# Row sums and row picks on the full TensorE array, padded with zeros, in a four-layer decoder trunk

## The chip, the cores and the metric

The kernel runs on one core of one Trainium2 chip. The metric is the device time of one execution in microseconds: 1587.0 us is the median of three executions of the kernel before (1582.32 to 1587.86). The profile is of one further execution.

## The reference

A decoder of four layers works on 16 learned tokens followed by 256 tokens (272 in all, in float32) with a model width of 1024. Layer i has the mixer of kind i mod 3, and after it a dense gated feed-forward part:

```
h = concatenate([meta, x])
for i in range(4):
    y = rmsnorm(h, norm_mix[i])
    mix = (fox, gla, gdn)[i % 3](y)
    h = h + mix
    h = h + swiglu(rmsnorm(h, norm_ffn[i]), w_gate_up[i], w_down[i])
return h[16:]
```

- `fox`, forgetting attention (layers 0 and 3): 16 heads of 64. Queries and keys are normed over their head, `q = rmsnorm(q) * 64**-0.5`, `k = rmsnorm(k)`. To each score is added `c[t] - c[s]`, where c is the running sum of `log_sigmoid(f + b)`. Then softmax, values, and a sigmoid gate.
- `gla`, gated linear attention (layer 1): 4 heads of 128 (values 256), decays for each channel, and `rmsnorm` of the output over each head times `silu(r)`.
- `gdn`, the delta rule (layer 2): 8 heads of 128, a short convolution, `l2norm` of queries and keys over the head, decays for each head, a triangular solve, and `rmsnorm` of the output over each head times `silu(gate)`.

What matters here are the sums of squares over a head, which become one number for each head and token, and the way these rows of numbers come back to 128 partitions.

## The kernel before, in words

Everything is held transposed: a tile has 128 channels on its partitions and the 272 tokens along it (`T = 272`). All weights stream once from memory, as units of 128 x 1024 (512 KB, eight blocks of 128 x 128), by DMAs on SP's queue (`load`, L372, `make_unit`, L552). ScalarE rounds each unit to the F32R type (`wh`), VectorE takes the rest (`wl`), and activations are split in the same way. A dense product is then three matmuls for each block, `wh*zh`, `wl*zh` and `wh*zl` (`block`, L529), each 128 x 128 by 272 columns, summed in one PSUM bank. There are 3360 blocks, and they are the bulk of TensorE's work.

Between the dense blocks run the small matmuls of the mixers. Each piece of work is a Python generator, started with `go` (L411). A planner (`turn`, L454, `step`, L490) keeps a modelled clock, `now`. At each step it takes the first generator whose operands are ready by the model, otherwise a dense block; that fixes TensorE's order, which `pe` (L382) writes into the program as a chain of dependencies. `mm` (L396) prices a matmul: for F32R its columns over 2400 a microsecond, for F32 four times that, or by the width of the weights if that is more. `pe` also counts columns, times `rhs.shape[0] / 128`, in steps of 3.413 us: with over 3060 in the last step the model is warm, otherwise prices double and dense blocks go first. Instructions of VectorE and ScalarE are ordered by the same clock (`Lane`, L206). A generator that yields a tile waits until the model has it done, and `bank` (L418) waits for a free PSUM bank, of which there are eight.

The small matmuls that this document speaks of:

- The sum over the model width (`norm_end`, L651, eight times): `ones`, a 128 x 128 constant of 1/1024, times the summed squares. Each of the 128 rows of the result holds the mean.
- Row sums over a head: squares of 128 x 272 (tile `sq`) are multiplied with a few columns of a strip that is zero but for one column (or two, a half each), so that the sum lands in row r of an accumulator; a window moved along the strip chooses r. They stand in `fox`, `qk_done` (L835, 8 columns of `strip2`, 16 for each layer), in `gla`, `out` (L1200, 8 columns of `strip1`, 8 in all) and in `gdn`, `row_sum` (L1368, for queries and outputs, 16 in all). Only those 8 rows of the bank are read afterwards. For keys, `k_done` (L1411) has the squares as the stationary operand, and one column of the strip moves.
- Picks: from a tile of rows (`ys`, `bs`, `cs`, `brs`: the upper half of a number in row h and its rest in row 32 + h, the others zero, from `rows_tile`, L703, and `hilo_rows`, L692) a stationary that is one in these rows (`pick`, L699: a column of the constant `sel`, broadcast along the columns) brings row h to all partitions. `fox` does it with `sel2` (L848) for two heads at once, `out_norm` (L1261) for the outputs of `gla` and `gdn`, where the tile lies in the buffer called `nacc`; `decay` in `gdn` (L1381, L1382) on 64 rows and 96 columns, in turn with two matmuls of `eye` and a mask on 96 x 96; `gram` (L1447) on 128 rows; `attend` (L886, L887) on either half of 128 rows of `cs`.
- Transposes (`tr`, L406) with the constant `ident`.

The trace calls all matmuls L403, all transposes L408 and all instructions of VectorE and ScalarE L244, so they are told apart by tiles (`out<-in`) and shapes. `con` is the tile of constants. One DMA brings it (L1741), the last but one of the loads at the start: a weight unit, `par`, four pieces of `h` with a second unit between them, `con`, a third unit.

Of the kernel before, what the change touches and what calls it, by code (L numbers as in the profile page):

```python
# [18 lines left out]
T = 272  # L19
# [119 lines left out]
def shape_consts():  # L139
    c = Cols()  # L140
    c.add("ident", np.eye(128))
    c.add("ones", np.full((128, 128), 1.0 / DM))
    strip = np.zeros((128, 30))
    strip[:64, 14] = 1.0 / 64
    strip[64:, 15] = 1.0 / 64
    c.add("strip2", strip)
    strip = np.zeros((128, 15))
    strip[:, 7] = 1.0
    c.add("strip1", strip)
    c.add("sel", np.tile(np.eye(32, 16), (4, 1)))  # L150
    return c

# [140 lines left out]
class Trunk:  # L293
# [357 lines left out]
    def norm_end(self):  # L651
        yield self.acc
        p = yield from self.bank()
        self.mm(p[:, :T], self.con("ones"), self.acc)
        self.v.tensor_scalar(self.ms, p[:, :T], EPS, None, ALU.add)
        self.free(p)
        yield from self.rsqrt(self.zp, self.rs, self.ms, rest=True)
        self.set(self.rs_ev)
# [41 lines left out]

        return self.sel[rows, h : h + 1].to_broadcast([rows.stop - rows.start, n])

    def rows_tile(self, pool, name, n=T, rows=64, bufs=None):  # L703
        st = pool.tile([128, n], F32R, tag=name, name=name, bufs=bufs)[:rows]
        self.v.tensor_scalar(st, self.con_t[:rows, 0:1].to_broadcast([rows, n]), 0.0, None, ALU.mult)
        return st
# [61 lines left out]
    def fox(self, j, lo, gain):  # L768
# [9 lines left out]
        with ExitStack() as cx:  # L778
# [41 lines left out]
            def qk_done(jp, which):  # L820
                grp, i = jp // GP, 2 * (jp % GP) + which

                def f(p):
                    raw = tp.tile([128, T], F32, tag=f"raw{i}", name="raw", bufs=2)
                    s.activation(raw, p[:, :T], AF.Copy)
                    sq = tp.tile([128, T], F32, tag="sq", name="sq", bufs=3)
                    s.activation(sq, p[:, :T], AF.Square)
                    self.free(p)
                    raws[jp, which] = raw
                    yield sq  # L830
                    if i == 0:
                        ssqs[grp] = yield from self.bank()
                    ssq = ssqs[grp]
                    n = 4 * GP
                    self.mm(ssq[:n, :T], self.con("strip2")[:, 14 - 2 * i : 14 + n - 2 * i], sq, i == 0, i == 2 * GP - 1)  # L835
                    if i == 2 * GP - 1:
                        mm = tp.tile([n, T], F32, tag="mm", name="mm")
                        v.scalar_tensor_tensor(mm, ms[:n], EPS, ssq[:n, :T], ALU.mult, ALU.add)
                        self.free(ssq)
                        y = tp.tile([n, T], F32, tag="y", name="y")  # L840
                        yield from self.rsqrt(self.zp, y, mm)
                        ys = self.rows_tile(tp, "ys")
                        self.hilo_rows(ys, y, 0)
                        yield ys
                        for i2 in range(2 * GP):
                            jq = grp * GP + i2 // 2
                            p = yield from self.bank()
                            self.mm(p[:, :T], self.sel2[:, i2], ys)  # L848
                            r = raws[jq, i2 % 2]
                            v.scalar_tensor_tensor(r, r, kg if i2 % 2 else qg, p[:, :T], ALU.mult, ALU.mult)  # L850
                            self.free(p)
                            if i2 % 2:
                                self.set(qk_ev[jq], r, raws[jq, 0])
                return f
# [124 lines left out]
    def gla(self, j, lo, gain):  # L979
# [4 lines left out]
        with ExitStack() as cx:  # L984
# [197 lines left out]
            def out(i):  # L1182
                yield at_ev
                yield v_ev[i]
                hd, grp = i // 2, i // GLA_GROUP
                p = yield from self.bank()
                for i3, (t0, n) in enumerate(TILES):
                    self.mm(p[:, t0:T], vsb[i3][:, i], at[i3][:n, hd, : T - t0], i3 == 0, i3 == 2)
                obs[i] = post[0].tile([128, T], F32, tag="ob", name="ob", bufs=KD)
                s.activation(obs[i], p[:, :T], AF.Copy)  # L1190
                self.set(o_ev[i], obs[i])
                yield from self.hold("sq", 3)
                sq = tp.tile([128, T], F32, tag="sq", name="sq", bufs=3)
                s.activation(sq, p[:, :T], AF.Square)
                self.free(p)
                yield sq
                if banks[grp] is None:
                    banks[grp] = yield from self.bank()
                r = hd % (GLA_GROUP // 2)
                self.mm(banks[grp][:8, :T], self.con("strip1")[:, 7 - r : 15 - r], sq, count2[grp] == 0, count2[grp] == GLA_GROUP - 1)  # L1200
                self.drop("sq")
                count2[grp] += 1
                if count2[grp] == GLA_GROUP:
                    self.set(s_ev[grp])
# [42 lines left out]
    def out_norm(self, new, tp, mm, ob, g_ev, oh_ev, tiles, row):  # L1247

        v = self.v
        y = self.zp.tile([128, T], F32, tag="nsq", name="y", bufs=2)[:8]  # L1250
        yield from self.rsqrt(self.zp, y, mm)
        ys = self.rows_tile(self.zp, "nacc", bufs=2)
        self.hilo_rows(ys, y, 0)
        for i in tiles:
            self.oh[i], self.ol[i] = new("oh"), new("ol")
        self.oh_ready = True
        yield ys
        for i in tiles:
            yield g_ev[i]
            p = yield from self.bank()  # L1260
            self.mm(p[:, :T], self.pick(slice(0, 64), row(i)), ys)  # L1261
            yield from self.hold("vt", 2)
            og = tp.tile([128, T], F32, tag="vt", name="og")
            v.tensor_mul(og, ob[i], p[:, :T])
            self.free(p)
            self.split(self.oh[i], self.ol[i], og)
            self.drop("vt")
            self.set(oh_ev[i], self.oh[i], self.ol[i])


    def gdn(self, j, lo, gain):
# [5 lines left out]
        with ExitStack() as cx:  # L1277
# [87 lines left out]
            def row_sum(name, i, sq):  # L1365
                if i % 4 == 0:
                    bank[name] = yield from self.bank()
                self.mm(bank[name][:8, :T], self.con("strip1")[:, 7 - i % 4 : 15 - i % 4], sq, i % 4 == 0, i % 4 == 3)  # L1368
                self.drop("sq")

            def decay():
# [6 lines left out]
                for i0 in range(0, H, GDN_DECAYS):  # L1378
                    ps = yield from self.bankn(GDN_DECAYS)
                    for i, p in enumerate(ps, i0):  # L1380
                        self.mm(p[:96, 0:T], self.pick(slice(0, 64), i, 96), bs, True, False)  # L1381
                        self.mm(p[:96, T:448], self.pick(slice(0, 64), i, 96), bs[:, 96:], False, False)  # L1382
                        self.mm(p[:96, 0:96], eye, dmask[:, 0:96], False, False)
                        self.mm(p[:96, T:448], eye, dmask, False, True)
                    for i, p in enumerate(ps, i0):
                        for out, c0, n, i3, kind in (
                            (d01[:, i, 0:96], 0, 96, 0, 0), (d01[:, i, 96:192], 96, 96, 0, 1), (d01[:, i, 192:272], 192, 80, 0, 2),
                            (d01[:, i, 272:368], 272, 96, 1, 0), (d01[:, i, 368:448], 192, 80, 1, 1), (d2[:, i], 368, 80, 2, 0)):
                            m = out.shape[0]
                            s.activation(out, p[:m, c0 : c0 + n], AF.Exp, bias=rc[:m, i3, 32 * kind + i : 32 * kind + i + 1])  # L1390
                        self.free(p)
                        self.set(d_ev[i], d01[:, i], d2[:, i])

            def k_done(i):
                def f(p):
# [12 lines left out]
                    if i == 0:  # L1408
                        bank["k"] = yield from self.bank()
                    for i3, (t0, n) in enumerate(TILES):  # L1410
                        self.mm(bank["k"][:n, 8 * i3 + i : 8 * i3 + i + 1], sq[:, t0 : t0 + n], self.con("strip1")[:, 7:8])  # L1411
                    self.drop("sq")
                    if i == H - 1:
                        pk = bank["k"]
# [304 lines left out]
    def run(self):  # L1719
        nc, tc = self.nc, self.tc  # L1720
        self.new_pools()
        with ExitStack() as cx:
# [6 lines left out]
            self.par_t = cp.tile([128, self.pcols.n], F32, name="par")  # L1729
            self.con_t = cp.tile([128, self.ccols.n], F32, name="con")  # L1730
            self.sel = cp.tile([128, 16], F32R, name="sel")
            self.sel2 = cp.tile([64, 4, 128], F32R, name="sel2")
            self.next_norm()
            self.nblock = 8 * 3
            self.make_unit()
# [10 lines left out]
            def start():  # L1746
                for k in range(KD):
                    self.norm_z(k, f"g_mix{self.layers[0][0]}")
                for k in range(KD):
                    self.norm_sum(k)  # L1750
                self.v.tensor_copy(self.sel, self.con("sel"))
                pairs = self.con("sel")[:64, 0:8].rearrange("p (i a) -> p i a", a=2)
                self.v.tensor_copy(
                    self.sel2.rearrange("p i (a b) -> p i a b", a=2), pairs[:, :, :, None].to_broadcast([64, 4, 2, 64]))
                yield from self.norm_end()

            self.go(start())
# [47 lines left out]
```

## Time and profile before

| what | value |
|---|---|
| median of three executions | 1587.0 us |
| profiled execution | 1581.87 us |
| its span, first to last instruction | 1580.1 us |
| granted TensorE clock, mean | 0.977 |
| instructions | 29533, of them 11985 matmuls |
| read from memory | 222.83 MB, 142 GB/s over the span |

The profile gives for each engine its busy time. "PE" is TensorE's matmuls, "PEld" its weight loads, "DVE" VectorE, "ACT" ScalarE, "POOL" GpSimd, "SP" the engine that issues the DMAs. The chain that ended last is followed back from the end, at each step to what released an instruction or to the instruction before it on its engine. In a line of a group or of the timeline, `128*8 128x272` means a stationary operand of 128 rows and 8 columns and a moving operand of 128 rows and 272 columns. Matmuls overlap, and their ends are modelled, so the cost of one is the distance between starts and not its length.

### The profile page before, as it was taken

How to read it: one execution, taken by the hardware profiler on the slowest of the kernel's cores; microseconds unless marked ns; L12 is line 12 of the kernel's file. 1: busy time of each engine (PE TensorE's matmuls, PEld its weight loads, DVE VectorE, ACT ScalarE, POOL GpSimd, SP SyncE). 2: the span in 40 equal slices, each digit the busy share in tenths (PEclk: the TensorE clock that was granted, in tenths of full speed). 3: DMA queues.
4: the chain of work that ended last, by engine and by line, in shares of the span. 5: the costliest groups of instructions: out<-in, count | busy, mean ns of one | idle time of the engine just before them, and what ended most of it. 6: DMA issues, size and time to landing. Idle time of an engine off the chain costs nothing.

```text
span 1580.1 us, 29533 instructions
## 1 busy us (share of the span) xinstructions
PE 1518.4 (96%) x11985; PEld 1443.8 (91%) x11985; DVE 1097.7 (69%) x2159; ACT 779.7 (49%) x1417; POOL 17.1 (1%) x56
## 2 busy tenths in 40 slices
PE   6999999999999999999895998999999999999999
PEld 6788999999998899999795887999999788999999
DVE  7677676665795776655879467876656777786653
ACT  5456554444445544444564344544444555654442
POOL 0000000000000000000100000000000000000000
PEclk9999999999999999999997899999999999999999
DMA  5232455555423455555332022455555323455564
GB/s 173 94 121 94 149 174 173 174 178 178 154 97 99 141 174 174 174 179 179 98 121 67 15 77 84 147 175 175 174 177 174 106 94 121 134 186 188 187 197 138
DMA packets 63897, 225.80 MB, mean 143 GB/s; under 512 B 7256, under 2 KB 9664, under 8 KB 63760
## 3 DMA queue, kind: packets, MB, share of 16 engines
q1 hardware_dynamic: 63760, 223.91, 43.9%
q8 instruction: 94, 1.54, 0.4%
q14 instruction: 43, 0.35, 0.1%
HBM read 222.83 MB, written 1.05 MB: 142 GB/s over the span
## 4 chain that ended last, share of the span: by engine, by line
PE 82%; DVE 8%; issue 5%; ACT 4%; DMA 1%; SPq 0%; POOL 0%; DVEq 0%; ACTq 0%; POOLq 0%
PE ps L403 81%; DVE wl L244 1%; PE ps L408 1%; ACT wh L244 1%; ACT pr L244 1%; DVE pr L244 1%; DMA w<-in_w_dram 1%; ACT d L244 1%; DVE sm L244 1%; DVE rq L244 1%; DVE tmp L244 0%; DVE ri L244 0%; DVE yc L244 0%; ACT pts L244 0%; DVE gx L244 0%
## 5 line engine op out<-in xcount | busy, mean ns | idle before, releaser
L403 PE MATMUL ps<-zh,wh 128*128 128x272 f32 (+1 forms) x2400 | 710.8, 296 | 12.4 <-ACT zh L244 10.1
L403 PE MATMUL ps<-zh,wl 128*128 128x272 f32 (+1 forms) x2400 | 697.0, 290 | 3.9 <-DVE wl L244 3.9
L403 PE MATMUL ps<-zl,wh 128*128 128x272 f32 (+1 forms) x2400 | 697.1, 290 | 0.0
L244 ACT ACTIVATE wh<-w 128x1024 fp32r<-128x1024 f32 x420 | 443.5, 1056 | 397.4 <-PE ps L403 232.5
L244 DVE TENSOR_TENSOR wl<-w,wh 128x1024 fp32r<-128x1024 f32 x420 | 512.2, 1221 | 166.8 <-ACT wh L244 166.5
L403 PEld LDWEIGHTS ps<-zh,wh 128*128 128x128 f32 x2400 | 458.9, 191 | 35.8 <-issue 17.9
L403 PEld LDWEIGHTS ps<-zh,wl 128*128 128x128 f32 x2400 | 458.9, 191 | 5.5 <-DVE wl L244 5.2
L403 PEld LDWEIGHTS ps<-zl,wh 128*128 128x128 f32 x2400 | 458.9, 191 | 0.3 <-DVE zl L244 0.2
L403 PE MATMUL ps<-al,wh 128*128 128x272 f32 (+1 forms) x704 | 202.0, 287 | 0.0
L403 PE MATMUL ps<-ah,wl 128*128 128x272 f32 (+1 forms) x704 | 201.3, 286 | 0.0
L403 PE MATMUL ps<-ah,wh 128*128 128x272 f32 (+1 forms) x704 | 200.7, 285 | 0.0
L403 PEld LDWEIGHTS ps<-ah,wh 128*128 128x128 f32 x704 | 133.0, 189 | 0.0
L403 PEld LDWEIGHTS ps<-al,wh 128*128 128x128 f32 x704 | 132.4, 188 | 0.0
L403 PEld LDWEIGHTS ps<-ah,wl 128*128 128x128 f32 x704 | 132.2, 188 | 0.0
L244 DVE TENSOR_TENSOR s<-t,rs 128x272 f32<-128x272 f32 (+1 forms) x88 | 38.5, 437 | 64.9 <-ACT t L244 64.7
L244 DVE TENSOR_TENSOR al<-a,ah 128x272 fp32r<-128x272 f32 (+1 forms) x88 | 38.6, 438 | 64.4 <-ACT ah L244 64.3
L403 PE MATMUL ps<-oh,wh 128*128 128x272 f32 (+1 forms) x256 | 75.5, 295 | 1.9 <-ACT wh L244 1.2
L403 PE MATMUL ps<-oh,wl 128*128 128x272 f32 (+1 forms) x256 | 74.9, 293 | 0.9 <-DVE wl L244 0.9
L403 PE MATMUL ps<-ol,wh 128*128 128x272 f32 (+1 forms) x256 | 74.7, 292 | 0.0
L244 ACT ACTIVATE ah<-a 128x272 fp32r<-128x272 f32 (+1 forms) x88 | 36.8, 418 | 62.8 <-DVE a L244 62.8
L244 ACT ACTIVATE zh<-h,par 128x272 fp32r<-128x272 f32 x64 | 32.6, 519 | 69.6 <-DVE h L244 68.9
L244 ACT ACTIVATE t<-t 128x272 f32<-128x272 f32 (+1 forms) x88 | 36.3, 416 | 37.1 <-DVE t L244 37.0
(224 smaller groups left out, 1499.6 us busy)
## 6 DMA issues: line engine op xcount, KB each, us to landing
w<-in_w_dram SPq DMA_DIRECT2D x420, 512.0 KB, 3.3
h<-in_h_dram SPq DMA_DIRECT2D x4, 272.0 KB, 4.9
out_dram<-h SPq DMA_DIRECT2D x8, 128.0 KB, 4.0
rst<-in_rst_dram SPq DMA_DIRECT2D x1, 576.0 KB, 5.4
mask<-in_fmask_dram SPq DMA_DIRECT2D x2, 210.0 KB, 5.4
con<-in_con_dram SPq DMA_DIRECT2D x1, 158.5 KB
mask<-in_gmask_dram SPq DMA_DIRECT2D x1, 126.0 KB, 3.1
par<-in_par_dram SPq DMA_DIRECT2D x1, 87.5 KB, 3.1
```

The source lines that it names most:

```text
L244: r = f(*args, **kw)
L403: ins = self.nc.tensor.matmul(out, lhsT, rhs, start=start, stop=stop)
L408: ins = self.nc.tensor.transpose(out, in_, self.con("ident")[:n, :n])
```

## The change

Row sums take a window of 128 columns of a longer strip in place of 8, and write all 128 rows of their bank; the added columns are zero. `strip1` and `strip2` become one strip of 270 columns. The picks of `ys` and `bs` take all 128 rows; their tiles are 128 partitions high, with zeros in the added rows, and `sel2` grows to 128 rows. The constant `ones` becomes one column, broadcast to 128. What is read from the results stays the same. The numbers of instructions, the loops and the prices in `mm` stay as they are; the constants are 415 columns where they were 317.

```diff
     c.add("ident", np.eye(128))
-    c.add("ones", np.full((128, 128), 1.0 / DM))
-    strip = np.zeros((128, 30))
+    c.add("ones", np.full((128, 1), 1.0 / DM))
+    strip = np.zeros((128, 270))
     strip[:64, 14] = 1.0 / 64
     strip[64:, 15] = 1.0 / 64
-    c.add("strip2", strip)
-    strip = np.zeros((128, 15))
-    strip[:, 7] = 1.0
-    c.add("strip1", strip)
+    strip[:, 142] = 1.0
+    c.add("strip", strip)
...
-        self.mm(p[:, :T], self.con("ones"), self.acc)
+        self.mm(p[:, :T], self.con("ones").to_broadcast([128, 128]), self.acc)
...
-    def rows_tile(self, pool, name, n=T, rows=64, bufs=None):
+    def rows_tile(self, pool, name, n=T, rows=128, bufs=None):
...
-                    self.mm(ssq[:n, :T], self.con("strip2")[:, 14 - 2 * i : 14 + n - 2 * i], sq, i == 0, i == 2 * GP - 1)
+                    self.mm(ssq[:, :T], self.con("strip")[:, 14 - 2 * i : 142 - 2 * i], sq, i == 0, i == 2 * GP - 1)
...
-                self.mm(banks[grp][:8, :T], self.con("strip1")[:, 7 - r : 15 - r], sq, count2[grp] == 0, count2[grp] == GLA_GROUP - 1)
+                self.mm(banks[grp][:, :T], self.con("strip")[:, 142 - r : 270 - r], sq, count2[grp] == 0, count2[grp] == GLA_GROUP - 1)
...
-            self.mm(p[:, :T], self.pick(slice(0, 64), row(i)), ys)
+            self.mm(p[:, :T], self.pick(slice(0, 128), row(i)), ys)
...
-                self.mm(bank[name][:8, :T], self.con("strip1")[:, 7 - i % 4 : 15 - i % 4], sq, i % 4 == 0, i % 4 == 3)
+                self.mm(bank[name][:, :T], self.con("strip")[:, 142 - i % 4 : 270 - i % 4], sq, i % 4 == 0, i % 4 == 3)
...
-                        self.mm(p[:96, 0:T], self.pick(slice(0, 64), i, 96), bs, True, False)
-                        self.mm(p[:96, T:448], self.pick(slice(0, 64), i, 96), bs[:, 96:], False, False)
+                        self.mm(p[:96, 0:T], self.pick(slice(0, 128), i, 96), bs, True, False)
+                        self.mm(p[:96, T:448], self.pick(slice(0, 128), i, 96), bs[:, 96:], False, False)
...
-                        self.mm(bank["k"][:n, 8 * i3 + i : 8 * i3 + i + 1], sq[:, t0 : t0 + n], self.con("strip1")[:, 7:8])
+                        self.mm(bank["k"][:n, 8 * i3 + i : 8 * i3 + i + 1], sq[:, t0 : t0 + n], self.con("strip")[:, 142:143])
...
-            self.sel2 = cp.tile([64, 4, 128], F32R, name="sel2")
+            self.sel2 = cp.tile([128, 4, 128], F32R, name="sel2")
...
-                pairs = self.con("sel")[:64, 0:8].rearrange("p (i a) -> p i a", a=2)
+                pairs = self.con("sel")[:, 0:8].rearrange("p (i a) -> p i a", a=2)
...
-                    self.sel2.rearrange("p i (a b) -> p i a b", a=2), pairs[:, :, :, None].to_broadcast([64, 4, 2, 64]))
+                    self.sel2.rearrange("p i (a b) -> p i a b", a=2), pairs[:, :, :, None].to_broadcast([128, 4, 2, 64]))
```

## The prediction

> **What bounds the kernel now.** I read the page first: busy shares, then the chain that ended last.
>
> ```profile
> PE 1518.4 (96%) x11985; PEld 1443.8 (91%) x11985; DVE 1097.7 (69%) x2159; ACT 779.7 (49%) x1417; POOL 17.1 (1%) x56
> ```
>
> ```profile
> PE 82%; DVE 8%; issue 5%; ACT 4%; DMA 1%; SPq 0%; POOL 0%; DVEq 0%; ACTq 0%; POOLq 0%
> ```
>
> TensorE is busy for 96% of the span and carries 82% of the chain, while VectorE is busy for 69%. So a microsecond taken from TensorE is a microsecond of the end, unless it is taken just ahead of a wait that ends on another engine. The view of waits, TensorE's alone, shows where those are.
>
> ```profile
> PE ps L403 <- DVE xm L244: 15.1, 1, 15.1
> PE ps L403 <- ACT zh L244: 10.1, 2, 6.3
> PE ps L403 <- ACT pts L244: 6.7, 12, 1.3
> PE ps L403 <- DVE ys L244: 6.6, 1, 6.6
> ```
>
> These four are 38.5 us, few and in known places: the triangular inverse in the delta layer (`xm`), a layer's new activations (`zh`), the attention of both forgetting-attention layers (`pts`), and the first query and key norm of all (`ys`). Most of the changed matmuls lie elsewhere. The view by tile, for the constants and for the selectors of the picks, gives what is changed (TensorE alone; shortest, median and longest ns, first and last start in us, shapes):
>
> ```profile
> L403 PE MATMUL ps<-sq,con x112: 392/393/661, 24.6 to 1326.7; 128*8 128x272 f32 x112
> ```
>
> ```profile
> L403 PE MATMUL ps<-ys,sel x32: 279/286/590, 39.4 to 1335.1; 64*128 64x272 f32 x32
> L403 PE MATMUL ps<-nacc,sel x16: 278/372/390, 509.6 to 987.3; 64*128 64x272 f32 x16
> L403 PE MATMUL ps<-bs,sel x16: 239/352/540, 780.0 to 788.2; 64*96 64x272 f32 x8, 64*96 64x176 f32 x8
> ```
>
> A shape is stationary rows by columns, then the moving operand. A row sum in F32 leaves two rows in the trace (56 calls, 112 rows), a pick in F32R leaves one. The durations do not show what a matmul costs here, because its end overlaps the next one. That is read from starts, in the timeline.
>
> **What a narrow matmul costs in the dense stream.** Four pieces of TensorE's timeline, each from the last dense matmul ahead of a small one to the second dense matmul behind it (columns: start, length, then the matmul):
>
> ```profile
> 66.11 0.29 PE L403 MATMUL ps<-zl,wh 128*128 128x272 f32 x1
> 66.33 0.63 PE L403 MATMUL ps<-sq,con 128*8 128x272 f32 x2
> 66.89 0.40 PE L403 MATMUL ps<-zh,wh 128*128 128x272 f32 x1
> 67.12 0.29 PE L403 MATMUL ps<-zh,wl 128*128 128x272 f32 x1
> 67.25 0.29 PE L403 MATMUL ps<-zl,wh 128*128 128x272 f32 x1
> ```
>
> ```profile
> 206.14 0.29 PE L403 MATMUL ps<-zl,wh 128*128 128x272 f32 x1
> 206.26 0.62 PE L403 MATMUL ps<-nacc,con 128*128 128x272 f32 x2
> 206.52 0.49 PE L403 MATMUL ps<-zh,wh 128*128 128x272 f32 x1
> 206.85 0.28 PE L403 MATMUL ps<-zh,wl 128*128 128x272 f32 x1
> ```
>
> Dense matmuls follow each other at 0.126 us (67.12 to 67.25). A row sum on 8 columns takes 67.12 - 66.11 = 1.01 us in this measure. The same arithmetic on the full 128 x 128 array, the norm's sum over the model width, takes 206.85 - 206.14 = 0.71. Both are F32, 272 columns long and wait for another engine's result; they differ in shape. So 0.30 us of each isolated row sum goes with the shape, some 0.09 on entry (66.11 to 66.33 against 0.126) and 0.2 on the way out. The picks show the same:
>
> ```profile
> 515.79 0.29 PE L403 MATMUL ps<-zl,wh 128*128 128x272 f32 x1
> 516.01 0.39 PE L403 MATMUL ps<-nacc,sel 64*128 64x272 f32 x1
> 516.33 0.39 PE L403 MATMUL ps<-zh,wh 128*128 128x272 f32 x1
> 516.56 0.29 PE L403 MATMUL ps<-zh,wl 128*128 128x272 f32 x1
> ```
>
> ```profile
> 815.98 0.29 PE L403 MATMUL ps<-zl,wh 128*128 128x272 f32 x1
> 816.10 0.41 PE L403 MATMUL ps<-brs,sel 128*128 128x272 f32 x2
> 816.35 0.29 PE L403 MATMUL ps<-zh,wh 128*128 128x272 f32 x1
> 816.48 0.29 PE L403 MATMUL ps<-zh,wl 128*128 128x272 f32 x1
> ```
>
> One pick on 64 rows takes 516.56 - 515.79 = 0.77. The kernel has a pick on 128 rows already (`brs`), with the same broadcast stationary: two take 0.50, 0.125 for each, so one would take 0.375. That is 0.39 us less. A full-array pick is as cheap as a dense matmul, stride-0 weights included, so the broadcast `ones` costs nothing either.
>
> Not every shape below 128 pays:
>
> ```profile
> 86.20 0.29 PE L403 MATMUL ps<-zl,wh 128*128 128x272 f32 x1
> 86.33 0.62 PE L408 MATMUL ps<-con,pr 96*96 96x96 f32 x6
> ```
>
> A transpose of 96 x 96 follows at the plain 0.13 us. So I count rows and columns in classes up to 32, up to 64 and above, and a price falls due where the class changes between two neighbours in TensorE's order.
>
> **The sum.** Going through all matmuls of the trace in order, the class changes 247 times; with row sums and picks made full, in the same order, 106 remain (the first that goes is at 24 us, the last at 1335). Of the 141 that go, 92 border a row sum, 33 a pick of `ys` or `nacc`, 16 a pick of `bs`. By the visits above, with two changes each, a change costs 0.15 us at a row sum and 0.195 at a pick. On TensorE that is 92 x 0.15 + 33 x 0.195 = 13.8 + 6.4 = 20.2 us without the decays.
>
> What of it reaches the end, by stage. (a) Three of the 125 lie before 40 us, ahead of the 6.6 us wait for `ys`, which hangs on VectorE: 0.5 us lost. (b) 29 lie in the first forgetting-attention layer, 26 in the gated linear one, 37 in the last layer; the first row below shows TensorE nearly full in the first of these, and what it waits for there (`pts`) starts from its own matmuls, so the waits move along; the other two are built alike in this. I count these in full.
>
> ```profile
> 45.00:165.00 120.00, 114.57 (x893) 96.52 (x893) 88.34 (x298) 70.22 (x190) 0.00 (x0) 0.99 0.31 98
> 865.00:995.00 130.00, 123.78 (x982) 106.46 (x981) 81.95 (x192) 57.46 (x147) 0.90 (x9) 0.89 0.17 54
> ```
>
> (The columns are busy time of TensorE, its weight loads, VectorE, ScalarE and GpSimd, the granted clock, and DMA.) (c) 30 lie in the second half of the delta layer, the second row: TensorE idles 6.2 us of 130 there and alternates with convolutions on VectorE. 30 changes are worth some 4.8 us; I take half as lost, 2.4, for want of a row that says which.
>
> (d) The 16 changes of the decays:
>
> ```profile
> 780.00 0.69 PE L403 MATMUL ps<-bs,sel 64*96 64x272 f32 x2
> ...
> 783.13 0.32 PE L403 MATMUL ps<-zh,wh 128*128 128x272 f32 x1
> ```
>
> ```profile
> 780.88 1.28 ACT L244 ACT_TABLE_LOAD   x1
> 782.17 2.55 ACT L244 ACTIVATE d<-ps,rc 96x96 f32<-96x96 f32 x11
> ```
>
> The first half of the decays keeps TensorE from 780.00 to 783.13, and could give back about 8 x 0.16 = 1.3 us, both halves 2.6. But the exponentials behind them start at 782.17, when ScalarE's table load ends, and run at 0.23 us each, six a head: 1.4 us a head against TensorE's 0.78 (3.13 over four heads). ScalarE sets the pace, so I count 0, with 2.6 as the other end.
>
> (e) What is added. The constants grow from 317 to 415 columns, 49 KB more in one DMA on SP's queue. What all queues moved in the first 30 us, and the first DMA of the chain:
>
> ```profile
> DMA packets 2929, 6.84 MB, mean 228 GB/s; under 512 B 272, under 2 KB 1552, under 8 KB 2928
> ```
>
> ```profile
> 4.66 7.12 DMA w<-in_w_dram
> ```
>
> At the 228 GB/s that the first 30 us moved it is 0.2 us, ahead of the weight unit at 4.66, whose landing begins the chain: I charge it in full. The wider zero fill, copies and evictions on VectorE keep their columns and gain only partitions: nothing. No instruction and no wait is added. Weight loads become longer:
>
> ```profile
> L403 PEld LDWEIGHTS ps<-zl,wh 128*128 128x128 f32 x2400 | 458.9, 191 | 0.3 <-DVE zl L244 0.2
> ```
>
> ```profile
> L403 PEld LDWEIGHTS ps<-sq,con x112: 85/88/93, 24.6 to 1326.5; 128*8 128x8 f32 x112
> ```
>
> Each row of a row sum will load some 191 ns instead of 88. That costs 0 if hidden, as in the norm's sum, whose 0.71 us has no room for two loads of 0.19 beside two dense steps of 0.126 and the sum itself; and 112 x 0.103 = 11.5 us if bare. I take 0: the norm's sum is the same instruction. The Trainium skill (TensorE: Matmul & The Clock Gate, Part 3, The mechanism) says that a weight load overlaps matmuls in flight only where its row group differs, and a full-height load shares its row groups with every matmul. By that the load would lie bare; Part 2 of the page also names a background weight buffer, which would hide it. The trace shows the second: dense matmuls, all of full height, start 0.126 us apart with loads of 191 ns, so loads do overlap.
>
> Together: 20.2 - 0.5 - 2.4 - 0 - 0.2 = 17.1 us. The profiled execution took 1581.87 us (its span is 1580.1), so 1564.8. The median of the three runs, 1587.0, lies 0.32% above it; on that footing 1570 us.
>
> **Rivals.** *Absorbed.* TensorE gains but VectorE and ScalarE end the same chains: softmax in both forgetting-attention layers (VectorE busy 88.34 of 120 us), convolutions in the delta layer. Then only the gated linear layer's 26 changes count, some 4.5 us: 1582. Against it: 82% of the chain on TensorE, and long waits for `xm` and `pts` that begin behind TensorE's work. Chance 0.10.
>
> *Another order.* The order is written by the planner. Its price of a matmul is unaffected (it counted no shape change and still does not), but it counts rows of the moving operand when it judges TensorE warm, and so doubles the picks, and its load of the constants is longer by 49 KB over its 360 GB/s, 0.14 us. Some small matmul may then stand a block sooner or later. One pick placed ahead of its operand costs a wait like that for `ys`: 6.6 us, giving 1577; two give 1583, and four a slower kernel at 1597. Chance of two or more 0.08, a quarter of it slower.
>
> *Bare loads, the other side.* If the excess of the row sums is a weight load that cannot be hidden (88 ns in each of two rows is more than half of 0.30), the padded ones pay 191: no gain at all, since the picks, which load 128 columns before and after, would keep their 0.77, and 11.5 us more. 1587.0 + 11.5 = 1598, slower. It decides from the point where a padded visit spans over 1.01 us. Against it stands the 0.71 of the norm's sum. The rule of the skill named above would make this case. Chance 0.05.
>
> *More than the sum.* The half lost in (c) and the decays also count: 20.2 - 0.5 + 2.6 - 0.2 = 22.1, so 1565; and if the 0.89 of granted clock in the delta window rises with fewer gaps to 0.94, 0.05 x 130 = 6.5 us more, 1558. Chance 0.05 for below 1560.
>
> **How the numbers follow.** About 0.5% (8 us) is what a measurement of this kernel can tell from no change; its three runs spread by 0.35%. The forecast, 1570, has 0.72: it covers 1560 to 1579. With the larger gain, faster has 0.77; absorbed and most of another order make 0.16 for no change; bare loads and the rest make 0.07 for slower. The range runs from 1558, the larger gain, to 1582, the absorbed case.
>
> **What would show it.** Right: visits of `sq,con` at 0.71 us and of single picks at 0.375, weight loads of 0.19 us for `sq,con`, some 106 class changes, TensorE's busy time about 17 to 20 us shorter, and the same long waits for `xm`, `zh`, `pts`. Wrong: padded visits still near 1.0 and 0.77 (the price is not the shape's); or visits shorter but idle time before `pts`, `vn`, `wl` or `wh` longer by as much (absorbed); or new waits on `ys` or `nacc` in a changed order.

## The result, and the profile after

The changed kernel takes 1562.07 us (median of four executions, 1560.04 to 1563.86), the kernel before 1587.43 us beside it (1582.32 to 1588.07): a ratio of 0.9847, with a 95% interval of 0.9823 to 0.9871. That is 24 us, and the interval reaches from 20 to 28. A second comparison gave less, 0.9886 (0.9870 to 0.9902), 18 us; it is told as the last experiment. Part of the difference lies in the kernel before: three of its four executions here took 1587.0 us or more, while the 69 beside the experiments have medians of 1583.1 to 1583.4. The forecast was 1570 us, 17 us less than before.

The profiled execution took 1560.04 us with a span of 1558.2 us. In it two lines of code are gone, so L401, L406 and L242 are what L403, L408 and L244 were before. The page, busy times:

```profile
PE 1496.0 (96%) x11985; PEld 1452.2 (93%) x11985; DVE 1096.6 (70%) x2159; ACT 778.9 (50%) x1417; POOL 17.2 (1%) x56
```

TensorE's busy time fell by 22.4 us with as many instructions, and its weight loads rose by 8.4. The other engines' work is what it was. The waits of TensorE, the longest:

```profile
PE ps L401 <- DVE xm L242: 15.1, 1, 15.1
PE ps L401 <- ACT zh L242: 9.5, 2, 6.4
PE ps L401 <- ACT pts L242: 8.1, 16, 1.3
PE ps L401 <- DVE wl L242: 6.3, 6, 1.5
```

The long ones (`xm`, `zh`) stand. Those on `pts` grew from 6.7 to 8.1 us; `wl` is new in the first four (it was 4.8 us), and the wait on `ys` has dropped out of them (2.7 us, from 6.6). The pieces of the timeline that answer to those of before, a row sum and a single pick:

```profile
67.02 0.29 PE L401 MATMUL ps<-zl,wh 128*128 128x272 f32 x1
67.15 0.62 PE L401 MATMUL ps<-sq,con 128*128 128x272 f32 x2
67.41 0.49 PE L401 MATMUL ps<-zh,wh 128*128 128x272 f32 x1
67.73 0.29 PE L401 MATMUL ps<-zh,wl 128*128 128x272 f32 x1
```

```profile
505.62 0.29 PE L401 MATMUL ps<-zl,wh 128*128 128x272 f32 x1
505.75 0.29 PE L401 MATMUL ps<-nacc,sel 128*128 128x272 f32 x1
505.87 0.29 PE L401 MATMUL ps<-zh,wh 128*128 128x272 f32 x1
506.00 0.29 PE L401 MATMUL ps<-zh,wl 128*128 128x272 f32 x1
```

The row sum now starts 0.13 us behind the dense matmul ahead of it, where it was 0.22, and the pick takes one dense step, 0.12 us, where the next dense matmul came 0.32 behind it. From start to start in the measure of the prediction, 14 isolated row sums span a median of 0.713 us (13 spanned 1.008 before), and 5 single picks 0.376 us (0.768). The weight loads of the row sums are 189 ns and do not show in this:

```profile
L401 PEld LDWEIGHTS ps<-sq,con x112: 186/189/193, 26.1 to 1304.5; 128*128 128x128 f32 x112
```

The order, however, is not that of before: of TensorE's 11985 matmuls 607 stand at another place. So two things changed, and the experiments take them apart.

### The profile page after: what moved, and what is told of

It is laid out like the page before. It is cut to its first block, busy times and chain, and to the rows that moved or that the text cites. A ratio compares the mean times of both kernels' runs of the same rounds, so it can differ in the third digit from the quotient of the medians.

```text
span 1558.2 us, 29525 instructions
## 1 busy us (share of the span) xinstructions
PE 1496.0 (96%) x11985; PEld 1452.2 (93%) x11985; DVE 1096.6 (70%) x2159; ACT 778.9 (50%) x1417; POOL 17.2 (1%) x56
## 3 DMA queue, kind: packets, MB, share of 16 engines
HBM read 222.88 MB, written 1.05 MB: 144 GB/s over the span
## 4 chain that ended last, share of the span: by engine, by line
PE 80%; DVE 9%; issue 5%; ACT 5%; DMA 1%; POOL 0%; SPq 0%; ACTq 0%; DVEq 0%; POOLq 0%
PE ps L401 80%; DVE wl L242 2%; ACT pr L242 1%; ACT wh L242 1%; DVE pr L242 1%; DVE sm L242 1%; DVE rq L242 1%; PE ps L406 1%; ACT d L242 1%; DVE ri L242 0%; ACT pts L242 0%; DVE tmp L242 0%; DMA h<-in_h_dram 0%; DMA w<-in_w_dram 0%; DVE gx L242 0%
## 5 line engine op out<-in xcount | busy, mean ns | idle before, releaser
L401 PE MATMUL ps<-zh,wh 128*128 128x272 f32 (+1 forms) x2400 | 712.6, 297 | 12.8 <-ACT zh L242 9.5
L401 PE MATMUL ps<-zh,wl 128*128 128x272 f32 (+1 forms) x2400 | 694.2, 289 | 5.4 <-DVE wl L242 5.4
L401 PE MATMUL ps<-zl,wh 128*128 128x272 f32 (+1 forms) x2400 | 695.9, 290 | 0.0
L242 ACT ACTIVATE wh<-w 128x1024 fp32r<-128x1024 f32 x420 | 443.5, 1056 | 388.7 <-PE ps L401 197.5
L242 DVE TENSOR_TENSOR wl<-w,wh 128x1024 fp32r<-128x1024 f32 x420 | 511.8, 1221 | 163.1 <-ACT wh L242 163.0
L401 PEld LDWEIGHTS ps<-zh,wh 128*128 128x128 f32 x2400 | 457.2, 191 | 22.8 <-ACT zh L242 9.7
L401 PEld LDWEIGHTS ps<-zh,wl 128*128 128x128 f32 x2400 | 457.4, 191 | 8.6 <-DVE wl L242 7.0
L401 PEld LDWEIGHTS ps<-zl,wh 128*128 128x128 f32 x2400 | 457.1, 190 | 0.3 <-DVE zl L242 0.2
L401 PE MATMUL ps<-al,wh 128*128 128x272 f32 (+1 forms) x704 | 202.0, 287 | 0.0
L401 PE MATMUL ps<-ah,wl 128*128 128x272 f32 (+1 forms) x704 | 201.3, 286 | 0.0
L401 PE MATMUL ps<-ah,wh 128*128 128x272 f32 (+1 forms) x704 | 200.7, 285 | 0.0
L401 PEld LDWEIGHTS ps<-ah,wh 128*128 128x128 f32 x704 | 133.0, 189 | 0.0
L401 PEld LDWEIGHTS ps<-al,wh 128*128 128x128 f32 x704 | 132.4, 188 | 0.0
L401 PEld LDWEIGHTS ps<-ah,wl 128*128 128x128 f32 x704 | 132.2, 188 | 0.0
L242 DVE TENSOR_TENSOR s<-t,rs 128x272 f32<-128x272 f32 (+1 forms) x88 | 38.4, 437 | 65.1 <-ACT t L242 64.8
L242 DVE TENSOR_TENSOR al<-a,ah 128x272 fp32r<-128x272 f32 (+1 forms) x88 | 38.6, 438 | 64.2 <-ACT ah L242 64.0
L401 PE MATMUL ps<-oh,wh 128*128 128x272 f32 (+1 forms) x256 | 75.4, 295 | 1.6 <-ACT wh L242 1.2
L401 PE MATMUL ps<-oh,wl 128*128 128x272 f32 (+1 forms) x256 | 75.2, 294 | 0.9 <-DVE wl L242 0.9
L401 PE MATMUL ps<-ol,wh 128*128 128x272 f32 (+1 forms) x256 | 74.9, 293 | 0.0
L242 ACT ACTIVATE zh<-h,par 128x272 fp32r<-128x272 f32 x64 | 32.7, 518 | 72.4 <-DVE h L242 71.4
L242 ACT ACTIVATE ah<-a 128x272 fp32r<-128x272 f32 (+1 forms) x88 | 36.8, 418 | 62.6 <-DVE a L242 62.6
L242 ACT ACTIVATE pr<-sm,mn 96x192 f32<-96x192 f32 (+3 forms) x96 | 42.2, 441 | 26.3 <-DVE mn L242 26.2
```

The source lines that it names most:

```text
L242: r = f(*args, **kw)
L401: ins = self.nc.tensor.matmul(out, lhsT, rhs, start=start, stop=stop)
```

## The experiments

Each was compared with the kernel before on its own chip. Microseconds are the ratio's distance from 1 times the median of before there (1583.1 to 1583.4 us). The last column is the clock that TensorE was not granted: one minus the granted clock, times the span, as the mean over a kernel's executions. Of the kernel before it is 37.0 us beside the first four kernels, 37.6 beside the next four and 37.8 beside the last four. The time goes with it: among the executions of the kernel before, each microsecond of it goes with about 0.8 us of time.

| kernel | ratio (95% interval) | us | clock not granted, us |
|---|---|---|---|
| shape_only | 0.9895 (0.9872 to 0.9918) | -16.6 | 29.7 |
| order_only | 0.9964 (0.9949 to 0.9979) | -5.7 | 33.6 |
| sums_only | 0.9946 (0.9925 to 0.9967) | -8.5 | 33.8 |
| picks_only | 0.9978 (0.9960 to 0.9996) | -3.5 | 36.4 |
| decay_only | 0.9984 (0.9968 to 0.9999) | -2.5 | 34.6 |
| order_load | 0.9937 (0.9920 to 0.9954) | -10.0 | 28.8 |
| order_cols | 0.9999 (0.9987 to 1.0011) | -0.2 | 38.6 |
| sums64 | 0.9983 (0.9971 to 0.9996) | -2.7 | 33.0 |
| ys_late | 1.0005 (0.9995 to 1.0016) | +0.8 | 36.0 |
| late_both | 0.9960 (0.9948 to 0.9973) | -6.3 | 36.2 |
| sums96 | 0.9931 (0.9914 to 0.9947) | -10.9 | 36.4 |
| full_again | 0.9886 (0.9870 to 0.9902) | -18.0 | 35.3 |

**Shape or order.** The planner sees two new numbers: the rows of the picks' moving operand, and the columns of the constants. `shape_only` makes the whole change but hands it the old ones, and its order is that of before; `order_only` makes nothing of the change but the numbers, and its order is that of the changed kernel. (In the trace of each pair two of the 11985 matmuls stand exchanged.)

```diff
-        self.pe(ins, cost, n * rhs.shape[0] / 128, (out, lhsT, rhs), max(self.done_at(lhsT), self.done_at(rhs)) + self.LAT)
+        self.pe(ins, cost, n * (64 if rhs.tensor.tag.startswith(("ys_","nacc_","bs_")) and lhsT.dtype == F32R else rhs.shape[0]) / 128, (out, lhsT, rhs), max(self.done_at(lhsT), self.done_at(rhs)) + self.LAT)
...
-        self.loaded = max(self.loaded, self.issued + 0.65) + max(0.2, out.free_size() * out.shape[0] * 4 / 360e3)
+        self.loaded = max(self.loaded, self.issued + 0.65) + max(0.2, (317 if out.name.startswith("con") else out.free_size()) * out.shape[0] * 4 / 360e3)
```

> All the padding, with the planner's inputs held at their old values, so that every engine's order is that of the kernel before. Theory A (the price of a shape change is all there is, and the decays and the second half of the delta layer count too): -20 to -25 us against before, nearly all of the changed kernel's -25. Theory B (the prediction's sum of 17 us was right for the shapes, and the other 8 us came from the new order): -15 to -19 us.

> No padding: the shapes of before, but the planner's inputs and so the order of the changed kernel. Theory A: within 3 us of before. Theory B: -6 to -10 us. A rival to both, that a new order costs time and the shapes give more than is seen: +3 us or more.

These lines are those of `shape_only`, beside the whole change; `order_only` has them with 128 and 415 in the kernel before. Shapes alone give 16.6 us (13 to 20), the order alone 5.7 (3 to 8). Theory B is the nearer: the shapes come to what the prediction's sum said, and the new order gains something in the kernel before, a little under the 6 us that B asks. Together they make 22 us, between the two measurements of the full change. That the rest of the first result is the order is not shown: `full_again`, below, has 1.4 us more than the shapes alone.

**The parts of the shape.** Each with the old order: all row sums with the strip and `ones` (`sums_only`), the picks of `ys` and `nacc` (`picks_only`), the picks of `bs` (`decay_only`). One pair of lines of each stands for all.

```diff
-                self.mm(bank[name][:8, :T], self.con("strip1")[:, 7 - i % 4 : 15 - i % 4], sq, i % 4 == 0, i % 4 == 3)
+                self.mm(bank[name][:128, :T], self.con("strip")[:, 142 - i % 4 : 270 - i % 4], sq, i % 4 == 0, i % 4 == 3)
...
-            self.mm(p[:, :T], self.pick(slice(0, 64), row(i)), ys)
+            self.mm(p[:, :T], self.pick(slice(0, 128), row(i)), ys)
...
-                        self.mm(p[:96, 0:T], self.pick(slice(0, 64), i, 96), bs, True, False)
+                        self.mm(p[:96, 0:T], self.pick(slice(0, 128), i, 96), bs, True, False)
```

> Only the row sums padded to 128 columns, in the order of before. 92 shape changes at 0.15 us: -10 to -14 us. If the row sums' weight loads of 0.19 us lay bare: +11 us. If price falls per visit with a pick beside it, less than 10.

> Only the picks of ys and nacc on 128 rows, in the order of before. 33 shape changes at 0.195 us: -5 to -6.5 us. If the excess came from the wait for VectorE's rows and not from the shape: 0.

> Only the 16 picks of the decays on 128 rows, in the order of before. By the prediction ScalarE's exponentials hide the gain: 0, within 1.5 us. If TensorE's time there reached the end: -2.5 to -3 us.

The sum of the three, 14.5, is near the 16.6 of all. Row sums give 8.5 us (5 to 12), under the 10 that was expected, picks 3.5 (1 to 6), also less; the last clause of the first expectation applies, and the section on the prediction shows why. The decays came to 2.5 us (0 to 5): the interval decides neither way, so the trace has to, below.

**Classes, or columns left out.** `sums_only` with windows of 64 and of 96 columns (one pair of lines of `sums64`):

```diff
-                self.mm(bank[name][:128, :T], self.con("strip")[:, 142 - i % 4 : 270 - i % 4], sq, i % 4 == 0, i % 4 == 3)
+                self.mm(bank[name][:64, :T], self.con("strip")[:, 142 - i % 4 : 206 - i % 4], sq, i % 4 == 0, i % 4 == 3)
```

> As sums_only, but the windows are 64 columns wide in place of 128. If the price is that of a change between classes (up to 32, up to 64, above), a sum of 64 columns pays as one of 8 does: a visit spans 1.0 us, and the time is that of before within 2 us. If the price falls in proportion to the columns left out, half of the gain of sums_only: -4 us and a visit of 0.85 us.

> As sums_only, but the windows are 96 columns wide. By classes (above 64 is as good as 128) a visit spans 0.71 us and the gain is that of sums_only, -8.5 us within 3. If the price falls with each column that is filled: three quarters of it and a visit of 0.78 us.

TensorE's timeline of `sums64` and of `sums96`, a lone row sum:

```profile
65.79 0.29 PE L403 MATMUL ps<-zl,wh 128*128 128x272 f32 x1
66.01 0.67 PE L403 MATMUL ps<-sq,con 128*64 128x272 f32 x2
66.61 0.40 PE L403 MATMUL ps<-zh,wh 128*128 128x272 f32 x1
66.84 0.29 PE L403 MATMUL ps<-zh,wl 128*128 128x272 f32 x1
```

```profile
71.54 0.29 PE L403 MATMUL ps<-zl,wh 128*128 128x272 f32 x1
71.67 0.62 PE L403 MATMUL ps<-sq,con 128*96 128x272 f32 x2
71.93 0.49 PE L403 MATMUL ps<-zh,wh 128*128 128x272 f32 x1
72.25 0.28 PE L403 MATMUL ps<-zh,wl 128*128 128x272 f32 x1
```

With 64 columns the sum starts 0.22 us behind its neighbour and spans 66.84 - 65.79 = 1.05 us, no less than the 1.01 of 8 columns. With 96 it starts at 0.13, and 13 such visits have a median of 0.708 us, as with 128. Of the columns, then, the price goes by class, with the step between 64 and 96. The times agree: 96 columns give 10.9 us (8 to 14), 64 columns 2.7 (1 to 5), a little beyond the 2 us that was allowed. The clock can account for the 2.7 (33.0 us not granted, from 37.6), but for only 1.4 of the 10.9 (36.4, from 37.8).

**What in the order.** The planner's two numbers one by one, with the shapes of before: `order_load` has only the 415 columns in `load`, `order_cols` only the 128 rows in `mm`.

```diff
+        self.loaded = max(self.loaded, self.issued + 0.65) + max(0.2, (415 if out.name.startswith("con") else out.free_size()) * out.shape[0] * 4 / 360e3)
```

> The shapes of before; of the planner's two new inputs only the longer load of the constants, which moves matmuls in the first layer's mixer alone. If the order's gain lies at the start, where the wait for ys falls from 6.6 to 2.5 us: -2 to -5 us, and 0 in the delta layer. If the gain at the start is chance: within 1.5 us.

> The shapes of before; of the planner's two new inputs only the doubled count of the picks' rows, which moves matmuls in the second half of the delta layer alone. If the order's gain lies there: about -3 us, and 0 at the start. If not: within 1.5 us.

The doubled rows do nothing by themselves (within 2 us). The 0.14 us more that the planner allows for the load of the constants give 10.0 us here (7 to 13), more than both numbers gave together in `order_only`, though the two intervals overlap. The expectation was wrong in one point: this number moves 181 matmuls of layer 0 (row sums, picks and attention among them), but also 307 of the delta layer. The profiled executions put 4.4 us of the gain in layer 0 and 2.9 in the delta layer behind its inverse (156.6 us before, 153.7 here). Such a split is rough: the changed kernel and `full_again`, the same instructions in the same order, took 179.9 and 183.0 us from norm to norm in layer 0, and 251.4 and 255.2 in the delta layer. Layer 0 from norm to norm, before and in `order_load` (length, then TensorE's busy time):

```profile
17.10:206.50 189.40, 177.39 (x1347) 156.59 (x1346) 141.18 (x398) 103.39 (x245) 0.00 (x0) 0.96 0.37 115
```

```profile
17.50:202.50 185.00, 176.66 (x1347) 155.88 (x1346) 141.45 (x399) 103.21 (x245) 0.00 (x0) 0.97 0.37 118
```

Idle time falls from 12.0 to 8.3 us. The most visible trace of it is the wait for `ys`, 6.6 us before and 2.6 here:

```profile
PE ps L403 <- DVE ys L244: 2.6, 1, 2.6
```

But most of the gain goes with the clock. The clock not granted falls from 37.6 to 28.8 us, 8.8 of the 10.0. All six executions of `order_load` were granted 0.980 or more, and none of the 29 of the kernel before beside them over 0.979. This counts the clock at its most: where TensorE waits for another engine, more clock need not shorten anything (the stage of the decays, below, went from 0.88 to 0.94 of the clock and grew by 0.5 us). In the traces the granted clock drops to a half for some stretches. The first one begins in the wait for `ys` in the kernel before (32.8 to 39.4 us), and behind that wait in `order_load`, where it is half as long. Before, then `order_load` (the clock is the third number from the end):

```profile
36.90:43.70 6.80, 4.30 (x17) 4.05 (x18) 6.60 (x14) 0.00 (x0) 0.00 (x0) 0.50 0.28 81
```

```profile
40.50:43.90 3.40, 3.40 (x14) 3.12 (x15) 3.40 (x6) 1.28 (x3) 0.00 (x0) 0.50 0.25 48
```

Why the new order is granted more clock was not tried by itself. The wait for `ys` was moved alone:

```diff
-                        yield ys
+                        yield ys if j + grp else max(self.done_at(ys) + self.LAT - self.now, 0.0) + 2.0
```

(`ys_late`; `late_both` is the same edit of the changed kernel.)

> The kernel before, with the planner told that the first four picks of ys are ready 2 us later, so that they and the fifth row sum stand 24 dense matmuls (3.0 us) later and little else moves. If the order's gain is that TensorE works on instead of waiting for ys: the wait falls from 6.6 to about 3 us, and the time by 3 to 10 us as in order_load. If it came from the two first heads standing apart behind it, which this kernel leaves together: within 2 us.

> The changed kernel with the same 2 us told to its planner: the first picks of ys stand 18 dense matmuls (2.3 us) later still. If the wait of 2.7 us that is left there can be filled: -26 to -28 us against before, 2 us under the changed kernel. If the picks now come too late for the softmax behind them: -20 to -24.

In `ys_late` nothing is gained, so the first of its two reasons fell as it was put. Its waits between 30 and 60 us:

```profile
PE ps L403 <- DVE wl L244: 6.1, 1, 6.1
PE ps L408 <- DVE mn L244: 1.5, 1, 1.5
PE ps L403 <- ACT pts L244: 0.8, 1, 0.8
```

The wait of 6.6 us for `ys` went, and one of 6.1 for the split weights `wl` came, on the same engine. TensorE waits there for VectorE, whichever of its results it asks for first. Since the time of waiting stayed, the run does not tell what a shorter wait is worth, and the second reason, the two first heads standing apart, is neither shown nor excluded. `late_both` met neither of its forecasts: it takes 12 us more than the changed kernel beside it. Most of its loss is not where the edit is. The stage of the gated linear layer, norm to norm, in `late_both` and then in `full_again` (columns as in the windows above):

```profile
402.30:554.40 152.10, 141.99 (x1124) 137.35 (x1123) 116.33 (x191) 76.21 (x129) 4.00 (x9) 0.97 0.36 115
```

```profile
398.90:543.00 144.10, 139.69 (x1132) 135.90 (x1130) 116.19 (x191) 75.37 (x130) 4.02 (x9) 0.99 0.38 121
```

It is 8.0 us longer, 5.7 of it idle time of TensorE (10.1 us against 4.4). A 2 us hint in layer 0 made the planner place small matmuls of layer 1 otherwise, 400 us later.

**The whole again.**

> The changed kernel's instructions and order once more, on the chip of the three others: -22 to -27 us against before, as shape_only and order_load add up.

18.0 us (15 to 21), less than was expected and less than the first comparison. The two intervals touch at 0.987. It is also only 1.4 us more than `shape_only` gave on the same chip, far within the intervals, and it was granted less clock (35.3 us not granted, 29.7 in `shape_only`). So what the new order is worth to the padded kernel is not shown.

## Why the prediction was right, point by point

**The price of a visit** was right: 0.71 and 0.375 us were forecast for the padded visits, 0.713 and 0.376 were measured, and rounding up to the class is what counts (`sums64`, `sums96`). Bare weight loads, the rival on the other side, are out: 189 ns a load, nowhere in the visit. By the rule of the Trainium skill weighed there (TensorE: Matmul & The Clock Gate, Part 3, The mechanism) they would have been seen; the measurement decides against it.

**The count times the price**, 20.2 us without the decays and 2.6 for them, was somewhat high. `shape_only` and the kernel before have the same order, so their intervals from start to start can be compared one by one (those over 0.48 us, which hold waits, left out). Around the changes at row sums they shrank by 11.1 us (13.8 forecast), at picks by 4.7 (6.4), at the decays by 2.9 (2.6). The price was taken from isolated visits; between small matmuls a change costs less. A row sum behind transposes, in `shape_only`:

```profile
83.95 0.29 PE L403 MATMUL ps<-zl,wh 128*128 128x272 f32 x1
84.08 0.62 PE L408 MATMUL ps<-con,pr 96*96 96x96 f32 x6
84.53 0.67 PE L403 MATMUL ps<-sq,con 128*128 128x272 f32 x2
84.83 0.49 PE L403 MATMUL ps<-zh,wh 128*128 128x272 f32 x1
85.16 0.28 PE L403 MATMUL ps<-zh,wl 128*128 128x272 f32 x1
```

This spans 85.16 - 83.95 = 1.21 us; before, that group ran from 86.20 to 87.67, 1.47 us, with two changes of 0.13 us each. Groups of four picks, three transposes and a row sum went from a median of 2.165 us to 1.755, four changes of 0.10.

**What reaches the end.** The windows from norm to norm, before and in `shape_only`: the last layer's attention, the delta layer behind its inverse, its first part with the decays, and the gated linear layer. The last line of the second block is layer 0 in `shape_only`; its line of before stands under the order, above.

```profile
1212.80:1394.20 181.40, 176.44 (x1398) 155.07 (x1397) 140.92 (x397) 105.46 (x246) 0.00 (x0) 1.00 0.37 120
858.40:1015.00 156.60, 150.35 (x1185) 133.02 (x1186) 103.92 (x231) 75.92 (x178) 1.00 (x10) 0.90 0.22 72
756.80:816.10 59.30, 54.59 (x397) 51.52 (x396) 46.35 (x98) 40.83 (x97) 0.88 (x11) 0.91 0.36 116
405.20:553.30 148.10, 143.36 (x1131) 134.57 (x1130) 116.16 (x191) 75.52 (x130) 4.01 (x9) 0.99 0.37 118
```

```profile
1198.10:1376.90 178.80, 171.84 (x1397) 158.91 (x1396) 140.84 (x397) 105.13 (x246) 0.00 (x0) 1.00 0.38 122
847.10:1000.30 153.20, 146.29 (x1184) 135.89 (x1185) 103.69 (x231) 76.07 (x178) 1.00 (x10) 0.90 0.22 73
745.00:804.80 59.80, 51.78 (x398) 50.15 (x397) 46.09 (x98) 40.73 (x97) 1.24 (x15) 0.94 0.36 115
399.10:541.80 142.70, 138.01 (x1131) 134.23 (x1130) 115.94 (x191) 75.77 (x130) 4.01 (x9) 1.00 0.38 122
17.70:200.40 182.70, 170.86 (x1347) 157.88 (x1346) 140.30 (x398) 102.76 (x245) 0.00 (x0) 0.98 0.38 119
```

Read the first two numbers behind the colon pair, the length and TensorE's busy time; their difference is its idle time. The third number from the end is the granted clock.

- (b), counted in full, was high in all three stages once the clock is counted. The gated linear layer is 5.4 us shorter with idle time unchanged (4.7), where 26 changes were to give some 4.3; but its granted clock is 0.99 before and 1.00 here, one stretch of 3.4 us at half clock, which is 1.7 us of the 5.4. Layer 0 went from 189.4 to 182.7 us, 6.7 where 4.6 were forecast; it holds two stretches of 6.8 us at half clock before and one here, 3.4 us of the 6.7. In the last layer, with a clock of 1.00 in both, (b) fails by half. TensorE's busy time falls by 4.6 us, but its idle time grows from 5.0 to 7.0, so 2.6 reach the end of some 6 forecast. There TensorE comes sooner to what VectorE and ScalarE have to give: its waits for `pts` grow from 2.9 to 3.5 us, those for `mn` and `wl` from 0.2 to 0.8 each. This is the rival *absorbed*, in one place.
- (c), half of 4.8 us lost in the delta layer, looks too careful: the stage is 3.4 us shorter at the same clock of 0.90, and idle time grows by 0.7. The 1 us between 2.4 and 3.4 is less than the changed kernel and `full_again`, one program, differ by there (149.6 and 151.7 us).
- (d), nothing from the decays, holds in the trace: TensorE is busy 2.8 us less and idle 3.3 us more, and the stage is 0.5 longer. In `decay_only` the same stage is 1.2 us shorter, and its time allows for anything from 0 to 5 us. Of its 2.5 us the clock can account for all (34.6 us not granted, from 37.6). So the wait takes most of the gain, and whether it takes all stays open.
- (e), the 0.2 us of the longer load, can't be seen. The first norm's sum comes 2.1 us later in the changed kernel (18.9 us, from 16.8), but as late in `decay_only`, whose constants are as small as before. What differs is how long TensorE starts slowly: dense matmuls start 0.227 us apart at first, 0.126 later, and the step comes at 10.6 us in the profile of before, at 14.6 in the changed kernel's. From 167.7 to 169.8 us of before, where the granted clock is 0.50, they also start 0.227 apart, so this is the clock. `full_again`, with the changed kernel's instructions, has the step at 10.7 us and the norm's sum at 16.9; so the 2.1 us do not come from the constants.

So 17.1 us met 16.6 in part by luck. TensorE's own gain outside the decays, 15.8 us, was put at 20.2, and the last layer's share of the end 3 us too high. On the other side stands the granted clock, which the sum has no term for; it stands only in the rival *more than the sum*, for the delta layer, where it stayed at 0.90 behind the inverse. The clock not granted is 29.7 us in `shape_only` and 37.0 in the kernel before beside it, so up to 7.3 of the 16.6 us go with it and at least 9.3 do not. Whether the padding itself brings the clock is not shown.

**The order** was named as a rival with losses only (6.6 us for each misplaced pick). In the kernel before it came as a gain, 5.7 and 10.0 us in two runs; that step was wrong in its sign. The gain hangs on the planner's load of the constants and goes for the larger part with the granted clock. In the padded kernel it is not shown. Which of the moved matmuls earn it stays open: the first two heads' attention standing apart, and the moves in the delta layer, were not tried alone.

## What to carry to other kernels

Where narrow matmuls stand singly in a stream of full ones, price them by the distance from the last full start to the second full start behind them, against the same matmul in full shape; if the full one is shorter, pad rows and columns with zeros (here rows to 128 and columns to 96 or 128; 64 columns gained nothing in a visit). Count neighbours that are narrow too at a lower price, and look in each stage for an engine that ends the same chain. If a planner writes the order, hold its inputs fixed to learn what an edit is worth: here the order moved the time by up to 12 us on changes of 0.14 and 2 us in what the planner was told. And set the granted clock beside each time, for a gain can be the clock's: up to 8.8 of the 10.0 us of `order_load`, up to 7.3 of the 16.6 of `shape_only`.

## What the runs showed of the hardware that was not expected

A stationary of 64 columns costs as much as one of 8 in the stream (1.05 and 1.01 us), one of 96 as little as 128 (0.71). The Trainium skill (TensorEngine Tiling (Array Packing), Tiling Modes and Key Properties) lists row and column tiles of 32, 64 and 128 and says that a change of mode drains TensorE; the classes and the 0.30 us of a row sum's visit agree with it, and its price, which the page does not give, falls to 0.10 to 0.13 us a change between small matmuls. A full-height weight load of 189 to 191 ns does not show between matmuls that start 0.126 us apart. And the granted clock, 0.50 in some stretches of 3.4 us and more, goes with several microseconds of the time: the 69 executions of the one kernel before, granted 0.973 to 0.980, took 1577.6 to 1588.7 us.
